# Softmax times values: who copies the last rows, when the last head's first bank is normalised, and how its scores are cut into loads

## The chip, the cores and the metric

The kernel runs on one core of one Trainium2 chip. The metric is the device time of one execution in microseconds (us), lower is better. A kernel is run several times and the median is given; executions differ by a few tenths of a microsecond, up to about one. The profile is one execution, with its own span from the first to the last instruction, 1.7 to 2.9 us below the device time of the same run.

Names of the engines: TensorE (PE in the profile, PEld for its weight loads), VectorE (DVE), ScalarE (ACT), GpSimd (POOL), and SyncE (SP), which issues all transfers.

## The reference

```python
def reference(scores, v):            # scores 8x12x1024x1024, v 8x12x1024x64, fp32
    scores_max = np.max(scores, axis=-1, keepdims=True)
    attn = np.exp(scores - scores_max)
    attn = attn / (np.sum(attn, axis=-1, keepdims=True) + 1e-8)
    return np.matmul(attn, v).astype(np.float32)
```

There are 96 heads (8 times 12), numbered 0 to 95 below. A head has 1024 rows of 1024 scores; the kernel handles them as 8 "rows" r = 0 to 7 of 128x1024 scores, half a megabyte each.

## The kernel before

A loop makes 24 passes of four heads, k = 0 to 3. The last pass has heads 92 to 95. For each row: ScalarE takes exp (no maximum is subtracted), TensorE transposes eight 128x128 blocks into PSUM (psT), VectorE copies them to SBUF (pt), and TensorE multiplies eight blocks by v, with a column of ones that gives the sums. Products run two rows behind the transposes (LAG). Four rows fill a PSUM bank; when it is full, VectorE inverts the sums and multiplies twice (two TENSOR_TENSOR, one for each half of the partitions).

```python
    def normalise(k, st, first, last):
        psO = psO_whole if k % 2 == 0 else psO_banks[first]
        ...
        nc.vector.reciprocal(out=recip, in_=psO[:, :, :, D : D + 1])
        for t in range(T):
            ...
            nc.vector.tensor_tensor(out=rows..., in0=psO[part, :, :, 0:D], in1=recip[part]..., op=mult)

    def finish(u):                       # the products of one row
        ...
        for c in range(C):
            nc.tensor.matmul(out=bank[:, g * M : (g + 1) * M], lhsT=pt[...], rhs=st["vones"][:, c, 0:M], ...)
        if k % 2 == 1:
            if g == G - 1:
                normalise(k, st, b, b + 1)
        elif r == R - 1:
            normalise(k, st, 0, R // G)
        ...

    def load_next(k, n0):
        if k < AHEAD - 2:
            load(k, (n0 + (AHEAD + k)) % BH, cond=n0 < BH - AHEAD)

    # last(n0), in the pass before the last: loads of heads 94 and 95, in parts of so many rows
                load(AHEAD - 2, BH - 2, (4, 4))
                load(AHEAD - 1, BH - 1, (2,))
                store(n0, AHEAD - T)
                load(AHEAD - 1, BH - 1, (2, 2, 1, 1), 2)

    # heads(n0), for every head k and row r
                if r % EB == 0:
                    rows = 1 if k == AHEAD - 1 and r == R - EB else EB      # EB = 2 rows in one exp
                    for g in range(0, EB, rows):
                        nc.scalar.activation(out=p_nat[...], in_=s_bufs[k][...], func=EXP)
                for c in range(C):
                    nc.tensor.transpose(out=psT[...], in_=p_row[...], identity=order16[:])
                pt = take(pt_bufs)
                nc.vector.tensor_copy(out=pt[:], in_=psT[:])
                pending.append((n0, k, r, pt, st))
                if len(pending) > LAG:
                    finish(pending.pop(0))
```

The softmax here doesn't subtract the row's maximum and nothing guards it: scores larger than these inputs give would overflow.

## Time and profile before

| what | value |
|---|---|
| device time, median of 3 runs (range) | 1064.57 us (1064.50 to 1064.79) |
| span of the profiled run | 1062.5 us |
| transfers | 453 MB in packets, mean 426 GB/s (HBM read and written: 461 MB, 434 GB/s over the span) |
| busy | ScalarE 69%, TensorE 68%, VectorE 64%, GpSimd 23% |
| last scores (row 7 of head 95) landed | 1052.02 us |
| first half of the last store issued | 1057.94 us |

How to read it: the transfers fill the span up to the last slice, so whatever an engine has to do before about 1050 us is hidden unless it reaches into the tail. A change that moves no bytes is worth only what it moves between the landing of the last scores and the last store. In the prediction below, L numbers are lines of the kernel; a timeline line gives start, busy time, engine, line, operation, output and input, and how often; in brackets the engine's idle time before it and what seems to have ended it.

### The profile page before, as it was taken

The page shows a single profiled execution, that of the slowest core. Times are in us where ns is not written, and L with a number is a line of the kernel's source. Part 1 is how long each engine was busy: PE and PEld are TensorE (multiplying, and loading weights), DVE is VectorE, ACT ScalarE, POOL GpSimd, SP SyncE. Part 2 cuts the span into 40 slices and gives each one's busy share as a digit, 9 for nine tenths or more (in the row PEclk, how much of TensorE's full clock was granted, in tenths as well). Part 3 has the DMA queues.
Part 4 walks back from the last instruction along what each step waited for, and adds up shares of the span by engine and source line. Part 5 has one row for each costly group of instructions (what it writes and reads, how often), then busy time and mean ns, then how long its engine had stood idle before and what let it go on. Part 6 is the DMA issues. An engine that isn't in the chain of part 4 may idle for free.

```text
span 1062.5 us, 32878 instructions
## 1 busy us (share of the span) xinstructions
PE 722.2 (68%) x12288; PEld 679.8 (64%) x12288; DVE 682.4 (64%) x1205; ACT 735.7 (69%) x432; POOL 243.5 (23%) x406
## 2 busy tenths in 40 slices
PE   2766766667766767666676666767667676667676
PEld 2765766657666667666676656757666576666675
DVE  1766666757566666666676656766667566666667
ACT  3766776666767668576675866767666677666686
POOL 3123212131121311212112221122121311203113
PEclk9888888888789798887888988888888988887989
DMA  9999999999999999999999999999999999999996
GB/s 398 429 418 434 429 434 434 432 435 432 431 429 432 430 432 435 434 433 432 435 424 434 433 429 435 427 441 433 432 432 427 433 429 435 434 433 433 432 427 257
DMA packets 25060, 453.06 MB, mean 426 GB/s; under 512 B 2784, under 2 KB 2784, under 8 KB 9312
## 3 DMA queue, kind: packets, MB, share of 16 engines
q1 hardware_dynamic: 25056, 453.00, 99.3%
q8 instruction: 4, 0.07, 0.0%
HBM read 436.21 MB, written 25.17 MB: 434 GB/s over the span
## 4 chain that ended last, share of the span: by engine, by line
DMA 61%; PE 15%; PEld 5%; ACT 5%; DVE 4%; issue 3%; POOL 3%; SPq 1%; POOLq 1%; ACTq 0%; PEldq 0%
DMA s_nat<-in_scores_dram 61%; PE psT L265 8%; PE psO L144 6%; ACT p_nat L253 5%; DVE pt L271 4%; PEld L265 3%; POOL vones L210 3%; PEld L144 2%; PE psO_whole L144 2%; SPq L201 1%; SPq L189 0%; POOLq L210 0%; POOLq L227 0%; POOLq L288 0%; POOLq L316 0%
## 5 line engine op out<-in xcount | busy, mean ns | idle before, releaser
L253 ACT ACTIVATE p_nat<-s_nat 128x2048 f16<-128x2048 f32 (+1 forms) x408 | 704.9, 1800 | 219.3 <-DMA s_nat<-in_scores_dram 192.2
L265 PE MATMUL psT<-order,p_nat 128*128 128x128 f16 x6144 | 565.0, 247 | 262.6 <-ACT p_nat L253 261.7
L271 DVE COPY pt<-psT 128x1024 f16<-128x1024 f16 x768 | 519.5, 690 | 348.4 <-PE L144 126.7
L265 PEld LDWEIGHTS <-p_nat 128*128 128x128 f16 x6144 | 448.6, 124 | 284.2 <-ACT p_nat L253 281.8
L210 POOL CAST vones<-v_sb 32x512 f16<-32x512 f32 x400 | 242.8, 607 | 815.9 <-PE L265 315.9
L144 PEld LDWEIGHTS <-pt 128*128 128x128 f16 x6144 | 303.9, 107 | 92.9 <-DVE pt L271 89.2
L144 PE MATMUL psO<-vones,pt 128*128 128x65 f16 x3072 | 183.2, 202 | 59.9 <-DVE pt L271 59.6
L144 PE MATMUL psO_whole<-vones,pt 128*128 128x65 f16 x3072 | 189.3, 209 | 12.3 <-DVE pt L271 11.9
L253 ACT ACT_TABLE_LOAD x24 | 30.8, 1283 | 98.5 <-DMA s_nat<-in_scores_dram 81.7
L128 DVE TENSOR_TENSOR out_sb<-psO,recip 64x256 f32<-64x256 f32 x192 | 81.2, 423 | 6.0
L128 DVE TENSOR_TENSOR out_sb<-psO_whole,recip 64x512 f32<-64x512 f32 x96 | 66.0, 688 | 3.1
L123 DVE RECIPROCAL recip<-psO 128x4 f32<-128x4 f32 x96 | 17.0, 177 | 17.2 <-PE psO L144 17.2
L123 DVE RECIPROCAL recip<-psO_whole 128x8 f32<-128x8 f32 x48 | 9.5, 198 | 0.0
L71 DVE MEMSET vones<- 128x16 f16 x4 | 0.2, 72 | 0.8 <-PEq L305 0.8
L62 DVE CAST order<-ident 128x128 f16<-128x128 f32 x1 | 0.2, 227 | 0.4 <-POOL ident masks.py:199 0.4
masks.py:199 POOL TENSOR_SCALAR_AFFINE_SELECT ident<-ident 128x128 f32<-128x128 f32 x1 | 0.3, 292 | 0.1
masks.py:197 POOL MEMSET ident<- 128x128 f32 x1 | 0.2, 204 | 0.3 <-POOLq L305 0.3
L305 POOL MEMSET const-float32-0.0<- 128x1 f32 x1 | 0.1, 98 | 0.3 <-issue 0.3
L305 POOL MEMSET const-bfloat16-1.0<- 128x1 bf16 x1 | 0.1, 100 | 0.0
L305 POOL MEMSET const-uint8-127<- 128x1 uint8 x1 | 0.1, 100 | 0.0
L305 POOL MEMSET const-float32-1.0<- 128x1 f32 x1 | 0.1, 98 | 0.0
## 6 DMA issues: line engine op xcount, KB each, us to landing
s_nat<-in_scores_dram SPq DMA_DIRECT2D x96, 4096.0 KB, 32.2
v_sb<-in_v_dram SPq DMA_DIRECT2D x24, 1024.0 KB, 18.4
out_dram<-out_sb SPq DMA_DIRECT2D x47, 512.0 KB, 27.6
s_nat<-in_scores_dram SPq DMA_DIRECT2D x2, 2048.0 KB, 33.4
s_nat<-in_scores_dram SPq DMA_DIRECT2D x3, 1024.0 KB, 27.4
s_nat<-in_scores_dram SPq DMA_DIRECT2D x2, 512.0 KB, 20.7
out_dram<-out_sb SPq DMA_DIRECT2D x2, 256.0 KB, 2.0
```

Source lines behind the costliest of these rows:

```text
L62: nc.vector.tensor_copy(out=order16[:].rearrange("p (t j) -> p t j", t=T), in_=ident32[:].rearrange("p (j t) -> p t j", t=T),)
L71: nc.vector.memset(vo[:, :, D : D + 2], 1.0)
L123: nc.vector.reciprocal(out=recip, in_=psO[:, :, :, D : D + 1])
L128: nc.vector.tensor_tensor(out=rows.rearrange("j (b g) d -> j b g d", g=G), in0=psO[part, :, :, 0:D], in1=recip[part].to_broadcast([W, last ...
L144: nc.tensor.matmul(out=bank[:, g * M : (g + 1) * M], lhsT=pt[:, c * P : (c + 1) * P], rhs=st["vones"][:, c, 0:M], start=(c == 0), stop=(c ...
L201: nc.sync.dma_start(out=v_sb[:].rearrange("x h s l d -> x (h s l d)"), in_=rows[bass.ds(n // AHEAD, 1)].rearrange("o x y -> (o x) y"),)
L210: nc.gpsimd.tensor_copy(out=vones_bufs[k][s * Q : (s + 1) * Q, :, 0:D].rearrange("i (h l) d -> i h l d", l=L), in_=v_sb[k * Q : (k + 1) * ...
L253: nc.scalar.activation(out=p_nat[:, g : g + rows, :].rearrange("p r (x v) -> p x r v", v=Q * L), in_=s_bufs[k][:, r + g : r + g + rows, :] ...
L265: nc.tensor.transpose(out=psT[:, c * P : (c + 1) * P], in_=p_row[:, c // L, c % L, :], identity=order16[:],)
L271: nc.vector.tensor_copy(out=pt[:], in_=psT[:])
L305: nc = _bacc.Bacc("TRN2", target_bir_lowering=False, num_devices=1)
```

## The change

Its intent is to shorten the tail. ScalarE, done with its exps, copies row 6 of a pass's last head, and VectorE is free for row 7's copy; the first bank of that head is normalised behind row 7's copy instead of ahead of it; and the very last head comes in parts of 3,2,1,1,1 rows, with exps of single rows from row 2 on.

```diff
-    def normalise(k, st, first, last):
+    def normalise(k, st, first, last, behind=None):
...
-        nc.vector.reciprocal(out=recip, in_=psO[:, :, :, D : D + 1])
+        inverse = nc.vector.reciprocal(out=recip, in_=psO[:, :, :, D : D + 1])
+        if behind is not None:
+            after(inverse, behind)
...
-            if g == G - 1:
+            if g == G - 1 and (b > 0 or k < AHEAD - 1):
                 normalise(k, st, b, b + 1)
...
-                load(AHEAD - 1, BH - 1, (2,))
+                load(AHEAD - 1, BH - 1, (3,))
                 store(n0, AHEAD - T)
-                load(AHEAD - 1, BH - 1, (2, 2, 1, 1), 2)
+                load(AHEAD - 1, BH - 1, (2, 1, 1, 1), 3)
...
-                    rows = 1 if k == AHEAD - 1 and r == R - EB else EB
+                    rows = 1 if k == AHEAD - 1 and r > 0 else EB
...
-                nc.vector.tensor_copy(out=pt[:], in_=psT[:])
+                if k == AHEAD - 1 and r == R - 2:
+                    nc.scalar.copy(out=pt[:], in_=psT[:])
+                else:
+                    copy = nc.vector.tensor_copy(out=pt[:], in_=psT[:])
+                if k == AHEAD - 1 and r == R - 1:
+                    normalise(k, st, 0, 1, copy)
```

## The prediction

> **What bounds the kernel now.** I read the page first: the slices of the span, the DMA queues, the waits of ScalarE; then only the last 15 us of the timeline.
>
> ```profile
> DMA  9999999999999999999999999999999999999996
> ...
> q1 hardware_dynamic: 25056, 453.00, 99.3%
> ...
> L253 ACT ACTIVATE p_nat<-s_nat 128x2048 f16<-128x2048 f32 (+1 forms) x408 | 704.9, 1800 | 219.3 <-DMA s_nat<-in_scores_dram 192.2
> ...
> out_dram<-out_sb SPq DMA_DIRECT2D x2, 256.0 KB, 2.0
> ```
>
> The 16 DMA engines are full in all slices but the last. In the packets I find no moment between 20 and 1045 us with fewer than 12 of the 16 at work. ScalarE, the busiest compute engine, is busy 69% and spends 192 us of its idle time waiting for scores. So 1045 us are set by 453 MB of traffic, and what compute does there has slack. The change moves no bytes. It can change the time only in what follows the last scores.
>
> The trace's landing records give the last head (number 95) in its parts of 2,2,2,1,1 rows: rows 0-1 complete at 1043.38 us, then the store of the heads before at 1044.69, rows 2-3 at 1047.13, rows 4-5 at 1049.54, row 6 at 1050.77, row 7 at 1052.02. A row takes 1.22 us. The span ends at 1062.5, so the tail after the last row is 10.5 us. The timeline there:
>
> ```profile
> 1049.64 3.81 ACT L253 ACTIVATE p_nat<-s_nat 128x2048 f16<-128x2048 f32 x3 [0.49 <-PE L265]
> 1050.82 0.69 DVE L128 TENSOR_TENSOR out_sb<-psO_whole,recip 64x512 f32<-64x512 f32 x1
> ...
> 1051.54 2.48 DVE L271 COPY pt<-psT 128x1024 f16<-128x1024 f16 x4
> ...
> 1053.94 0.18 DVE L123 RECIPROCAL recip<-psO 128x4 f32<-128x4 f32 x1
> ...
> 1054.24 0.69 DVE L271 COPY pt<-psT 128x1024 f16<-128x1024 f16 x1
> ...
> 1054.96 0.88 DVE L128 TENSOR_TENSOR out_sb<-psO,recip 64x256 f32<-64x256 f32 x2
> ...
> 1055.87 0.69 DVE L271 COPY pt<-psT 128x1024 f16<-128x1024 f16 x1
> 1056.61 0.31 PEld L144 LDWEIGHTS <-pt 128*128 128x128 f16 x8 [1.32 <-DVE pt L271]
> ...
> 1057.28 0.18 DVE L123 RECIPROCAL recip<-psO 128x4 f32<-128x4 f32 x1 [0.72 <-PE psO L144]
> 1057.49 0.88 DVE L128 TENSOR_TENSOR out_sb<-psO,recip 64x256 f32<-64x256 f32 x2
> ```
>
> What to see: ScalarE is done with its last exp at 1049.64+3.81 = 1053.45. From 1050.1 on VectorE runs without a pause: it normalises head 94 (until 1051.51), then copies rows 2 to 5, inverts bank 0, copies row 6 (1054.24), multiplies bank 0 (1054.96 to 1055.84), and only then copies row 7 (1055.87). TensorE waits 1.32 us for that copy. Row 7's product, its normalising and a store follow, then the fixed teardown. VectorE, not the last exp, sets the tail: row 7's transposes have long been there (their slice ends at 1054.36). The releaser named for the exp at 1049.64 is a matmul that had long ended; it is row 5's landing at 1049.54.
>
> **What the Trainium skill says.** "ScalarE: Activation LUTs", section "What ACT_TABLE_LOAD costs", gives an ACTIVATE with immediates 186 ns + 0.833 ns an element and an overlap of 93 ns back to back: 1039 ns at 1024 elements. The trace has 1043 ns for the exp of one row, and 1051.46 to 1052.41 between two starts, 0.95, so it agrees. Its section "Table sets" has copy in every set, so the new copy should need no table load; the built instruction list indeed has one load per pass, as before.
> "VectorE: DVE Perf Modes", "Side-by-side": a 16-bit copy at two elements a cycle is (512+8+150)/0.96 = 698 ns; the trace has 690. So a copy on ScalarE costs 0.35 us more than on VectorE, but beside it.
> "PSUM — Partial Sum Buffer", "Specifications", lets both engines read PSUM at full rate in different banks. Rows 6 and 7 lie in different transpose buffers of one bank each; no run yet shows it.
> "DMA: Bandwidth & Descriptors", "Anatomy of one DMA", has some 2 us of fixed cost; the last 256 KB stores take 2.0 from issue to landing. That stays.
>
> **The change part by part.**
> 1. Parts of 3,2,1,1,1, and exps of one row from row 1 pair onward (six where two were). Rows 0-2 complete at 1043.38+1.22 = 1044.60; the exp of rows 0-1 starts at 1044.67 today because ScalarE is busy until then, so nothing is lost. Rows 3-4 land at 1044.69+1.22+2.44 = 1048.35, row 5 at 1049.57, rows 6 and 7 as before. Exp of row 2 runs 1046.5 to 1047.5; row 3 starts at 1048.45; rows 4, 5, 6, 7 follow every 0.95, at 1049.40, 1050.35, 1051.30, 1052.25, the last ending at 1053.29. Gain against 1053.45: 0.16, and not on VectorE's chain.
> 2. ScalarE copies row 6, after its last exp. VectorE loses one 0.69 copy.
> 3. The inverse and the two products of bank 0 (0.18 + 0.88) move from ahead of row 7's copy to behind it.
> 4. In the built order VectorE now copies row 2 between the inverse and the products of head 94. That copy, and row 7's, wait for VectorE's own previous instruction; today such copies (row 6 of this head, for one) start 0.12 to 0.27 after the one before, the others 0.09 before its end.
>
> VectorE's new chain, from 1050.07, where head 94's inverse ends now as then: row 2's copy 1050.19 to 1050.88; two products of 0.69, 1050.91 to 1052.32; rows 3, 4, 5 at 1052.35, 1052.95, 1053.55, ending 1054.24 (today the same work ends at 1054.02: +0.22). Row 7's copy needs its transposes, and TensorE takes them in fixed order behind the product of row 4, which waits for row 4's copy (1053.65): product from 1053.71, transposes from 1053.96, and 0.71 from the first transpose to the copy (1023.63 to 1024.34 in the timeline): 1054.67. It ends at 1055.36, against 1056.56 today: 1.20 gained. Then bank 0, now exposed: inverse 1055.28 to 1055.46, products to 1056.37. Row 7's product starts at 1055.41 and releases the inverse 0.66 later (1056.62 to 1057.28 today) at 1056.07, so VectorE is later: inverse of bank 1 at 1056.40, first product 1056.61 to 1057.03. Today it ends at 1057.91. The gain is 0.88: 1.20 minus 0.32 in which bank 0 outlasts row 7's product.
> ScalarE's copy: row 6's transposes are split round the product of row 3, which waits for row 3's copy (1053.04): done about 1053.75, copy 1053.8 to 1054.85, product from 1054.9, 0.5 before row 7's. It is beside the path.
> The first of the two last stores is issued as its product ends, the second 0.68 later by the queue's pace, landing 2.0 after; both shift by 0.88, as does the teardown (VectorE's and GpSimd's ends move along). 1064.57 - 0.88 = 1063.69.
> In the 23 other passes ScalarE gets one more copy and three more starts, about 1.3 us, where it waits 3.45 us for scores at the start of each next pass: zero.
>
> **Rivals.**
> A. The copy of row 7 is bound by its exp alone: ending at 1053.29, transposes from 1053.35, copy at 1054.05, bank 0 done by 1055.8; a gain near 1.5, 1063.1. For it: the change aims at this. Against: VectorE is solid from 1050.1, and head 94's products still stand before row 3.
> B. ScalarE's copy takes the place of the removed wait: it stands behind the last exp and row 6's late transposes. It has 0.5 of slack before row 7's product, and 0.33 more since VectorE comes later; only a copy above 1.8 us would cost. At 2.5 us the gain would be near 0.2: 1064.4.
> C. The tail shifts but the span doesn't, as another chain ends last: GpSimd's four casts end at 1060.02, released by the last product, which shifts 1.2. They end before the stores (1060.67) and still will.
> D. The extra work at the end of each pass delays the loads or adds 0.1 us a pass: +2, 1066. Against: three loads queued, 32.2 us from issue to landing, with 9.7 us for one.
>
> **Range and chances.** The sum says 1063.7. Half of the gain rests on VectorE gaps of 0.1 to 0.3 us, so +-0.4; runs differ by 0.3; rival A stretches the low side. Range 1063.1 to 1064.4. 2% are 21 us, twice the whole tail, so "within 2%" is nearly sure.
>
> **What would show it right or wrong.** Loads landing within 0.2 of 1052.0; row 7's copy on VectorE starting near 1054.7 (1054.0 would be rival A); ScalarE's copy near 1.04 us with no table load; the two inverses within 1.2 us of each other; first last store issued near 1057.1. Wrong would be a DMA gap before 1045, or TensorE waiting for ScalarE's copy ahead of its last product.

## The result, and the profile after

The changed kernel took 1064.22 us (median of 6 runs, 1063.69 to 1064.56), the kernel before in the same rounds 1064.59 us (6 runs, 1064.39 to 1064.93). The ratio is 0.9996, with a 95% interval of 0.9983 to 1.0009. (Ratios here are the mean time of one kernel's fast runs over that of the other's of the same rounds, so not quite the ratio of the medians.) That is "same", inside the predicted range, but the difference of the medians is 0.37 us where 0.88 had been summed up. A second set, told below, gave 0.33. Neither set is clear of noise by its interval.

Spans scatter less: from span to device time it is anything from 1.73 to 2.86 us, in runs of one and the same kernel. In the three later calls the kernel before has spans of 1062.5 to 1063.8 us (27 runs, median 1062.7). The changed kernel has 1061.9 to 1062.5 in the first set (6 runs, median 1062.1) and 1062.0 to 1063.1 in the second (5 runs, median 1062.2, where the kernel before has 1062.8 in the same call; four of the five lie below all nine of it). So a gain of some 0.5 to 0.6 us stands out of the scatter of the spans, and the traces show where it comes from.

The page of the changed kernel: the same lines as before, and the new copy on ScalarE.

```profile
DMA  9999999999999999999999999999999999999996
...
q1 hardware_dynamic: 25056, 453.00, 99.4%
...
L255 ACT ACTIVATE p_nat<-s_nat 128x2048 f16<-128x2048 f32 (+1 forms) x456 | 709.4, 1630 | 218.6 <-DMA s_nat<-in_scores_dram 192.2
...
L275 ACT COPY pt<-psT 128x1024 f16<-128x1024 f16 x24 | 24.3, 1012 | 44.9 <-PE psT L267 21.7
...
out_dram<-out_sb SPq DMA_DIRECT2D x2, 256.0 KB, 2.0
```

The transfers are as they were, ScalarE still waits 192.2 us for scores, and its new copies of 1012 ns cost nothing outside the tail. Row 7 of the last head landed at 1052.05 us, against 1052.02.

Its timeline in the tail:

```profile
1050.60 0.69 DVE L277 COPY pt<-psT 128x1024 f16<-128x1024 f16 x1 [0.15 <-PE L146]
...
1051.32 1.41 DVE L130 TENSOR_TENSOR out_sb<-psO_whole,recip 64x512 f32<-64x512 f32 x2
...
1052.76 1.88 DVE L277 COPY pt<-psT 128x1024 f16<-128x1024 f16 x3
...
1054.44 1.01 ACT L275 COPY pt<-psT 128x1024 f16<-128x1024 f16 x1 [1.11 <-PE L267]
...
1055.40 0.69 DVE L277 COPY pt<-psT 128x1024 f16<-128x1024 f16 x1 [0.76 <-PE psO L146]
...
1056.01 0.17 DVE L123 RECIPROCAL recip<-psO 128x4 f32<-128x4 f32 x1
...
1056.21 0.88 DVE L130 TENSOR_TENSOR out_sb<-psO,recip 64x256 f32<-64x256 f32 x2
...
1057.12 0.18 DVE L123 RECIPROCAL recip<-psO 128x4 f32<-128x4 f32 x1
1057.34 0.88 DVE L130 TENSOR_TENSOR out_sb<-psO,recip 64x256 f32<-64x256 f32 x2
```

The order is the predicted one: row 2, head 94's products, rows 3 to 5 (ending at 1054.64), row 7, bank 0, bank 1. But the reader is to see the 0.76 us in the row 7 line. VectorE is idle from 1054.64 to 1055.40, in the middle of what had been taken for its own chain, and it is TensorE that it waits for. Row 7's copy starts 0.47 us earlier than in the kernel before (1055.87), not 1.20. And nothing stands between the products of bank 0 and the inverse of bank 1 (1056.21+0.88 = 1057.09, then 1057.12): bank 0, moved behind the copy, now delays bank 1. The first half of the last product ends at 1057.75, against 1057.91 before.

**Where TensorE really is.** Ends of matrix multiplies in a profile are modelled. The trace has something firmer: every matrix multiply and every weight load counts up a semaphore when it is done, and the time of each count is recorded. Set beside the timeline for a row's eight transposes (us, worked out from the trace's semaphore records):

```
                       slices in the timeline   last transpose counted   copy starts
before, row 7 of 95      1053.75 to 1054.36            1055.18             1055.87
after,  row 0 of 95      1047.59 to 1048.23            1048.72             1048.74
after,  row 1 of 95      1048.29 to 1048.90            1049.62             1049.64
after,  row 2 of 95      1048.99 to 1049.61            1050.58             1050.60
after,  row 7 of 95      1054.37 to 1054.98            1055.38             1055.40
```

The four copies of the changed kernel start 0.02 us after the last count: they wait for TensorE, which is up to 1.2 us further behind than its slices look. (The recorded texts below have these counts 0.03 earlier: they were read one count short. That the sixteenth count of a row is the one is seen where TensorE has stood idle before a row: in the kernel before, the first count after the pause at 1023.63 us is at 1023.75, the sixteenth at 1024.31, and the copy starts at 1024.34.) The counts never come closer than 0.029 us in the whole trace. In full clock they come every 0.030, so a load and its multiply take 0.060, a row's transposes and products (16 pairs) 0.96 us. Between 1038.2 and 1055.0 us, 560 counts of 0.030 would fit; the changed kernel has 560, the kernel before 554. In the changed kernel TensorE is saturated from there to its last product, without a pause in its counts. In the kernel before it pauses twice: 0.18 us at 1051.64, for an exp of two rows, and 0.64 us at 1056.13, for VectorE's copy of row 7. Whether the array or the counting sets this pace, the traces do not tell.

**A second thing that the timeline hides**: TensorE's clock. The view by windows, of the kernel before:

```profile
core 0: us, PE busy (x) PEld busy (x) DVE busy (x) ACT busy (x) POOL busy (x), PEclk, DMA share, GB/s
1022.93:1029.77 6.84, 5.74 (x90) 5.48 (x91) 4.22 (x8) 6.06 (x4) 2.22 (x4) 0.75 0.95 405
```

and of the changed kernel, the same stretch:

```profile
1022.93:1029.77 6.84, 6.07 (x68) 5.91 (x69) 3.44 (x6) 6.12 (x4) 1.32 (x3) 0.50 0.96 408
```

The column to read is the granted clock after the engines: 0.75 and 0.50. TensorE runs at half clock for windows of 3.4 or 6.8 us, which fall differently in every run. Here one of 6.8 us ended at 1029.8 in the changed kernel, one of 3.4 us at 1027.6 in the kernel before, and so 68 multiplies were begun in the stretch instead of 90. The lost time reaches the tail, because TensorE has no pause in which to catch up.

I therefore measure every tail from two marks: the landing of head 93, 22 us before the last row's, and the end of TensorE's last pause before its saturated stretch, which I call its entry (to be exact, the second count after that pause). It comes 7.82 us after that landing in the kernel before and 8.17 after it in the changed kernel. From entry to the end of the first product of bank 1 (the moment the first half of the last store can go), the kernel before takes 20.13 us and the changed one 19.60. So the change gained 0.53. Row 7's copy comes 0.85 us earlier from entry: 0.67 for which VectorE had held it back behind its finished transposes (1055.87 less 1055.18, less the 0.02), and 0.18 by which TensorE no longer pauses at 1051.64. Of that, bank 0 takes 0.28 back behind the last product. And the profiled run gave 0.35 back at entry, after its longer half-clock window.

### The profile page after: what moved, and what is told of

Read it like the earlier page. It is cut to its first block, busy times and chain, and to the rows that moved or that the text cites. A ratio compares the mean times of both kernels' runs of the same rounds, so it can differ in the third digit from the quotient of the medians.

```text
span 1062.5 us, 33096 instructions
## 1 busy us (share of the span) xinstructions
PE 722.9 (68%) x12288; PEld 677.3 (64%) x12288; DVE 664.5 (63%) x1181; ACT 764.5 (72%) x504; POOL 244.2 (23%) x406
## 4 chain that ended last, share of the span: by engine, by line
DMA 62%; PE 16%; ACT 5%; PEld 5%; issue 3%; POOL 3%; DVE 3%; SPq 1%; POOLq 1%; ACTq 0%; DVEq 0%
DMA s_nat<-in_scores_dram 62%; PE psT L267 8%; PE psO L146 6%; ACT p_nat L255 5%; POOL vones L212 3%; PEld L267 3%; DVE pt L277 3%; PEld L146 2%; PE psO_whole L146 1%; SPq L203 1%; SPq L191 0%; POOLq L212 0%; POOLq L229 0%; POOLq L297 0%; POOLq L325 0%
## 5 line engine op out<-in xcount | busy, mean ns | idle before, releaser
L255 ACT ACTIVATE p_nat<-s_nat 128x2048 f16<-128x2048 f32 (+1 forms) x456 | 709.4, 1630 | 218.6 <-DMA s_nat<-in_scores_dram 192.2
L277 DVE COPY pt<-psT 128x1024 f16<-128x1024 f16 x744 | 502.8, 690 | 382.6 <-PE L146 117.6
L146 PE MATMUL psO<-vones,pt 128*128 128x65 f16 x3072 | 178.4, 202 | 41.0 <-DVE pt L277 29.6
L275 ACT COPY pt<-psT 128x1024 f16<-128x1024 f16 x24 | 24.3, 1012 | 44.9 <-PE psT L267 21.7
```

What stands on the lines that cost most here:

```text
L146: nc.tensor.matmul(out=bank[:, g * M : (g + 1) * M], lhsT=pt[:, c * P : (c + 1) * P], rhs=st["vones"][:, c, 0:M], start=(c == 0), stop=(c ...
L255: nc.scalar.activation(out=p_nat[:, g : g + rows, :].rearrange("p r (x v) -> p x r v", v=Q * L), in_=s_bufs[k][:, r + g : r + g + rows, :] ...
L275: nc.scalar.copy(out=pt[:], in_=psT[:])
L277: copy = nc.vector.tensor_copy(out=pt[:], in_=psT[:])
```

## The experiments

Theory T: TensorE's pace from head 93's landing bounds the tail. Theory V: VectorE's chain does, as the prediction had it. Three calls of the chip, each with its own runs of the kernel before (medians 1064.54, 1064.71 and 1064.65 us, 9 runs each). One table for all; "entry" is measured from the landing of head 93, the other three from entry, in us. Outputs are right except in the two kernels marked wrong.

| kernel | median (range) us | last half-clock window ended | entry | row 7's copy | last product counted | bank 1's first product ends |
|---|---|---|---|---|---|---|
| before | 1064.59 (1064.39 to 1064.93) | 1027.6 | 7.82 | 18.09 | 19.48 | 20.13 |
| after | 1064.22 (1063.69 to 1064.56) | 1029.8 | 8.17 | 17.24 | 18.66 | 19.60 |
| parts_only | 1064.56 (1064.30 to 1065.16) | 1028.0 | 7.83 | 18.10 | 19.49 | 20.14 |
| undo_copy | 1063.94 (1063.79 to 1065.04) | 1029.1 | 8.02 | 17.24 | 18.66 | 19.60 |
| undo_order | 1063.96 (1063.77 to 1064.73) | 1028.4 | 7.82 | 17.53 | 18.91 | 19.57 |
| relief_after (wrong) | 1063.51 (1063.25 to 1064.26) | 1026.7 | 7.82 | 16.74 | 18.15 | 19.10 |
| after_again | 1064.38 (1063.78 to 1064.87) | 1026.7 | 7.83 | 17.24 | 18.66 | 19.60 |
| split_after | 1064.67 (1064.64 to 1065.41) | 1029.6 | 7.82 | 17.24 | 18.66 | 19.60 |
| split_undo_order | 1064.98 (1064.45 to 1065.50) | 1029.7 | 7.82 | 17.52 | 18.91 | 19.56 |
| burden_after (wrong) | 1067.61 (1066.84 to 1067.93) | 1028.5 | 7.88 | 19.16 | 20.58 | 21.52 |
| lag3_after | 1064.00 (1063.66 to 1064.54) | 1029.6 | 8.09 | 16.82 | 18.66 | 19.32 |
| lag3_undo_order | 1063.97 (1063.63 to 1065.26) | 1028.3 | 7.82 | 16.82 | 18.66 | 19.32 |

split_before (1065.70 us, 1065.39 to 1065.82) has no such pause and is told in its own place.

### relief_after: less for TensorE

```diff
-        for c in range(C):
+        chunks = C // 2 if k == AHEAD - 2 else C
+        for c in range(chunks):
...
-                stop=(c == C - 1),
+                stop=(c == chunks - 1),
```

> The changed kernel, but head k=2 of each pass takes four of its eight products a row (a wrong result on purpose): 32 matrix multiplies, by the 0.060 us that the semaphore records put between two, 1.92 us less of TensorE in the last pass ahead of the last head, no VectorE, ScalarE or DMA work less. Theory T (TensorE's own rate bounds the tail: it completes without a pause from about 1043 to 1056.8 us and row 7's copy waits for row 7's transposes): row 7's copy starts about 0.6 us after the last exp ends instead of 2.1, the first of the last stores is issued 1.0 to 1.5 us earlier after the last landing, time 1062.7 to 1063.3. Theory V (the prediction's: VectorE's chain of copies and products bounds it): the chain starts no earlier, gain under 0.3, time 1063.9 to 1064.3.

Wrong on purpose, and measured 1063.51 us: between the two ranges, so both missed by the clock. In the trace, row 7's copy starts 1.26 us after the last exp ends (2.08 in the changed kernel), the first product of bank 1 ends 0.50 earlier after entry, and the first of the last stores goes 0.85 us earlier after row 7's landing (4.88 against 5.73). Taking work from TensorE alone shortens the tail, for which theory V allowed under 0.3 us, and VectorE stands idle for 1.59 us before row 7's copy; but only 0.50 of the 1.92 us taken away shows, because TensorE then pauses 1.4 us more than in the changed kernel, for exps and copies. The other engines are close behind.

### undo_copy: row 6 back to VectorE

```diff
-                if k == AHEAD - 1 and r == R - 2:
-                    nc.scalar.copy(out=pt[:], in_=psT[:])
-                else:
-                    copy = nc.vector.tensor_copy(out=pt[:], in_=psT[:])
+                copy = nc.vector.tensor_copy(out=pt[:], in_=psT[:])
```

> The changed kernel with row 6 copied by VectorE again. Theory T: row 7's transposes complete no earlier or later; VectorE has row 6's copy done about 0.2 us after they are, so row 7's copy and all behind it shift by 0.3 to 0.5 us: about as slow as before, 1064.4 to 1064.7. Theory V: VectorE's chain gets 0.69 plus a gap of 0.27 longer, about 0.5 to 0.9 us lost, 1064.7 to 1065.1.

Both theories had this slower; it was not (1063.94 us). The timeline:

```profile
1053.06 1.88 DVE L273 COPY pt<-psT 128x1024 f16<-128x1024 f16 x3
...
1055.09 0.69 DVE L273 COPY pt<-psT 128x1024 f16<-128x1024 f16 x1 [0.15 <-PE L146]
```

VectorE makes rows 4, 5 and 6 in one stretch, without the gap that I had put before row 6, ends at 1054.94, and still waits 0.15 us for row 7's transposes (counted at 1055.07). From entry, every column of the table is that of the changed kernel. ScalarE's copy bought nothing: it fills a time in which VectorE would have been idle.

### undo_order: bank 0 where it was

```diff
-            if g == G - 1 and (b > 0 or k < AHEAD - 1):
+            if g == G - 1:
                 normalise(k, st, b, b + 1)
...
-                if k == AHEAD - 1 and r == R - 1:
-                    normalise(k, st, 0, 1, copy)
```

> The changed kernel with the first bank normalised where it was, ahead of row 7's copy; ScalarE still copies row 6. Theory T: the 1.06 us of inverse and products fit between row 5's copy (end 1054.65) and row 7's transposes (complete 1055.35) but for about 0.3 us, and bank 0 no longer stands between the last product and its inverse: within 0.15 us of the changed kernel, 1064.1 to 1064.3. Theory V: row 7's copy starts 0.7 us later, the end is 0.3 to 0.5 us later: 1064.5 to 1064.7.

1063.96 us, faster than either theory said, and 19.57 against 19.60 from entry: the same, as theory T has it. Row 7's copy is 0.29 us later, since bank 0's products stand before it, and the last product 0.25 later; but the inverse of bank 1 then follows that product by 0.02 us instead of 0.30. What the order wins at one end it loses at the other.

### parts_only: the kernel before with the new parts and exps

```diff
-                load(AHEAD - 1, BH - 1, (2,))
+                load(AHEAD - 1, BH - 1, (3,))
                 store(n0, AHEAD - T)
-                load(AHEAD - 1, BH - 1, (2, 2, 1, 1), 2)
+                load(AHEAD - 1, BH - 1, (2, 1, 1, 1), 3)
...
-                    rows = 1 if k == AHEAD - 1 and r == R - EB else EB
+                    rows = 1 if k == AHEAD - 1 and r > 0 else EB
```

> The kernel before with only the parts of 3,2,1,1,1 rows and the exps of one row from the second pair on. Theory T and theory V alike: the last exp ends 0.1 to 0.2 us earlier, but row 7's copy still stands behind row 6's copy and the first bank's products, and row 2's copy takes a gap of 0.2 more: 0 to 0.2 us slower than before, 1064.6 to 1064.8. If the parts are the gain: 1064.2.

1064.56 us beside 1064.54 of the kernel before; from entry 20.14 and 20.13. The last exp does end earlier after row 7's landing (1.29 us against 1.43), and nothing comes of it. By themselves the parts are neutral. They do take away TensorE's pause of 0.18 us (row 7's transposes are counted 17.22 us after entry, as in the changed kernel, and 17.40 in the kernel before), but behind VectorE's chain that doesn't show. The change without the new parts was not run; it may lack these 0.18 us.

So with the new parts in place, row 6 on VectorE and bank 0 ahead of row 7 together cost 0.5 us; taking away either is worth all of it, and the second adds nothing.

### after_again: the changed kernel once more

> The changed kernel once more, for the spread and for another phase of TensorE's half-speed windows. Measured from row 7's landing, the first half of the last store's product ended at 5.70 in the first profile, in which the last half-speed window ended at 1029.8 us. Theory T: TensorE is behind by what such a window leaves over; if the window ends before 1028.5 the product ends at 5.3 to 5.45, if after 1029.5 at 5.6 to 5.75. If phase has no part in it, 5.7 again. Time 1063.7 to 1064.5.

1064.38 us beside 1064.71. The half-clock window ended at 1026.7 this time, the product ended 5.15 us after row 7's landing (5.70 in the first profile). That is under the expected 5.3 to 5.45, because the last row itself landed late (1052.47), which is why I changed to measuring from entry: entry is 7.83 instead of 8.17, and from entry all four columns are equal to the first profile's to 0.01 us. What goes with entry over the twelve profiles of the table is how long before head 93's landing the last window ended: where it was 1.2 us or more, entry is 7.82 to 7.88 (split_after and split_undo_order are among these, as head 93 landed later there); where it was 0.7, 0.4 and 0.2 us, in undo_copy, lag3_after and after, entry is 8.02, 8.09 and 8.17. That is a pattern, not an experiment: nothing here sets the windows.

### split_before, split_after, split_undo_order: an earlier start for head 92

```diff
-            load(k, (n0 + (AHEAD + k)) % BH, cond=n0 < BH - AHEAD)
+            parts = (R // 2, R // 2) if k == 0 else (R,)
+            load(k, (n0 + (AHEAD + k)) % BH, parts, cond=n0 < BH - AHEAD)
```

> The kernel before with the scores of head k=0 of each pass loaded in two parts of four rows, so that in the last pass its exps start at about 1018 us instead of 1021.7 and TensorE doesn't pause 2 to 3 us between 1020.8 and 1025.7. Nothing else changes, outputs stay right. Theory T: TensorE is 1 to 2 us ahead when the last head comes; row 7's copy then stands behind VectorE's chain alone: first product of bank 1 ends 5.0 to 5.4 after row 7's landing instead of 5.9, time 1063.7 to 1064.2. Theory V: nothing in the tail starts earlier, 1064.4 to 1064.8. If the extra transfer a pass costs DMA time: over 1065.

> The changed kernel with the same two parts for head k=0. Theory T: with TensorE out of the way the change has the effect that the prediction summed up: row 7's copy 2.2 to 2.6 after row 7's landing (3.35 without the parts), the product ends at 4.5 to 4.9, time 1063.0 to 1063.5, 0.5 to 0.9 under split_before. If ScalarE's copy at the end of a pass holds up the exps of the next head (it ended at 1020.24 in the changed kernel), the lead is 1 us smaller than in split_before and the gain under 0.4. Theory V: same as the changed kernel, 1064.0 to 1064.4.

> As split_after, with bank 0 normalised ahead of row 7's copy as before the change. Theory T: row 5's copy ends about 1053.1, bank 0 is done by about 1054.3, row 7's copy starts 2.3 to 2.6 after row 7's landing, and after its product only bank 1 is left: product ends at 4.2 to 4.6, time 1062.7 to 1063.2, the best of all. Theory V as in the prediction's step 3: 0.3 to 0.4 slower than split_after.

1065.70, 1064.67 and 1064.98 us: outside the ranges of both theories in all three; only the branch "over 1065" of split_before came true. Two things were wrong in the theories' ranges. First, the extra transfer of every pass is not free: head 93 landed at 1030.9 us and row 7 at 1052.9 to 1053.0, some 0.8 later than in most other profiles, although the same bytes moved and no moment between 20 and 1045 us has fewer than 12 packets in flight. The packet records show where it went: a packet of 32 KB took 1.214 us on average, two of 16 KB 1.222, and the packets' times come to 1057.5 to 1057.7 us on each of 16 engines, against 1055.4 in the kernel before and 1055.7 and 1056.0 in the two profiles of the changed one. Second, the lead is not kept. In split_before the exps of head 92 do start at 1019.15 instead of 1021.66, but ScalarE and TensorE then just wait for head 93, which still comes whole: TensorE's counts pause for 1.2 us at 1031.95. (A half-clock window, 1034.3 to 1037.8 us, also fell into the stretch that leads to its tail.) In split_after there is no lead at all: ScalarE's copy of the pass before ends at 1020.56, and the exps of head 92 start behind it at 1022.05, no earlier than without the split. It and split_undo_order have an entry of 7.82 and the columns of the kernels without the split, so they tell nothing new of the tail. What split_before shows is that a lead on head 92 alone is given back while TensorE waits for head 93. Splitting head 93 too was not run: I expected the next pass's first load to wait for the last store then, which no run here shows.

### burden_after: more for TensorE

```diff
-        for c in range(C):
+        chunks = list(range(C)) + (list(range(C // 2)) if k == AHEAD - 2 else [])
+        for i, c in enumerate(chunks):
...
-                start=(c == 0),
-                stop=(c == C - 1),
+                start=(i == 0),
+                stop=(i == len(chunks) - 1),
```

> The changed kernel, but head k=2 of each pass takes four of its products a second time (a wrong result on purpose): 32 more matrix multiplies a pass, 1.92 us of TensorE at 0.060 each, nothing for VectorE, ScalarE and DMA. Theory T, now from head 93's landing on (TensorE has no pause worth naming from 2 us after that landing to its last product): the first product of bank 1 ends 29.3 to 29.7 us after head 93's landing instead of 27.4 (27.8 with a late half-speed window), time 1.6 to 2.0 over the changed kernel, 1065.9 to 1066.3. Theory V: VectorE has not a copy more to make, under 0.3 later, 1064.2 to 1064.6.

Wrong on purpose. From entry, the last product comes 1.92 us later (20.58 against 18.66), the very 32 pairs of 0.060, and bank 1's product 1.92 later (21.52 against 19.60). From head 93's landing it is 29.40 us, inside theory T's 29.3 to 29.7. VectorE's line for row 7:

```profile
1058.49 0.69 DVE L278 COPY pt<-psT 128x1024 f16<-128x1024 f16 x1 [1.11 <-PE psO L147]
```

VectorE has no copy more to make and is idle for 1.11 us before this one, again for TensorE. This is the run that decides between the theories for the changed kernel. The time, 1067.61 us, is 1.3 above what I had expected, because head 93 landed at 1031.44 us, 1.2 to 1.6 later than in the profiles without a split; why the longer products delay the loads of the passes before is left open.

### lag3_after and lag3_undo_order: row 7's transposes first

```diff
-                if len(pending) > LAG:
+                if len(pending) > (LAG + 1 if k == AHEAD - 1 and r > R // 2 else LAG):
```

> The changed kernel with the products of the last head three rows behind its transposes from row 5 on, not two, so that row 7's transposes come ahead of seven of row 4's eight products. The same instructions, only their order on TensorE. Theory T: TensorE's last product ends as before, 26.5 after head 93's landing, but row 7's copy starts 0.42 earlier and bank 0 is done when the last product is: the product of bank 1 ends 27.05 to 27.25 after head 93's landing instead of 27.42 (27.4 to 27.6 with a late window), time 0.2 to 0.4 under the changed kernel, 1063.8 to 1064.1. Theory V: row 7's copy follows VectorE's chain, which is unchanged: 0.0 to 0.1.

> As lag3_after with bank 0 normalised as before the change (its inverse comes ahead of row 7's copy, its products behind). Theory T: VectorE has the same work in the same 1.9 us between row 7's transposes and the last product, so the same within 0.1 us of lag3_after: 27.05 to 27.3 after head 93's landing.

The same instructions in another order on TensorE. Measured 1064.00 and 1063.97 us beside 1064.65. From entry the last product is where it was (18.66), row 7's copy 0.42 earlier (16.82), and bank 1's product ends at 19.32, 0.28 earlier, whichever way bank 0 goes. From head 93's landing that is 27.41 in lag3_after (entry 8.09 behind a late window) and 27.14 in lag3_undo_order, both as expected. The timeline of the latter:

```profile
1054.73 0.69 DVE L277 COPY pt<-psT 128x1024 f16<-128x1024 f16 x1 [0.24 <-PE L146]
1055.45 0.88 DVE L130 TENSOR_TENSOR out_sb<-psO,recip 64x256 f32<-64x256 f32 x2
...
1056.59 0.18 DVE L123 RECIPROCAL recip<-psO 128x4 f32<-128x4 f32 x1 [0.26 <-PE psO L146]
1056.81 0.88 DVE L130 TENSOR_TENSOR out_sb<-psO,recip 64x256 f32<-64x256 f32 x2
```

Row 7's copy and bank 0 are both done, and VectorE waits 0.26 us for the last product. This is the shortest tail of all kernels with right outputs, and it has come down to TensorE's stream and one bank's normalising. By the clock it is 0.7 us under the kernel before, which its interval (ratio 0.9996, 0.9983 to 1.0010) does not separate from zero, and level with undo_copy and undo_order. By the spans it is clear: 1061.7 to 1062.9 us (5 runs, median 1062.0) beside 1062.5 to 1062.9 (9 runs, median 1062.7), four of the five below all nine.

## Why the prediction was right or wrong

The time fell into the predicted range, near its upper end, and in part by luck: the range had room for any gain from 0.2 to 1.5 us, and the step that was to bring most of the 0.88 failed. What failed is TensorE's part in it.

- **Nothing but the tail matters: right for the transfers, wrong for TensorE.** What compute does before 1045 us was said to have slack, but TensorE has none from 1038 us on, and its backlog reaches the tail. The DMA rows of both pages agree, row 7 landed within 0.03 us, and the copies in the 23 other passes cost nothing. There ScalarE's slack turned out smaller than I had it: in the last pass but one the copy ended at 1020.24 and the next scores landed at 1020.31.
- **"VectorE, not the last exp, sets the tail: row 7's transposes have long been there (their slice ends at 1054.36)": this is the step that failed.** They were counted as done at 1055.18, and TensorE had been all but saturated for 17 us by then. The slices show modelled ends, and I took one for a fact. VectorE did set the tail of the kernel before, but of its hold on row 7's copy only 0.67 us was there to be won; then TensorE sets it, as it does in the changed kernel.
- **Row 7's copy at 1054.67, "0.71 from the first transpose to the copy": wrong.** It took 1.03 (1054.37 to 1055.40), because TensorE had a backlog. The 0.71 came from 1023.63 us, where it had just been idle. From entry, the copy gained 0.85 us where 1.20 was forecast, and the first last store was issued at 1057.78, not near 1057.1. Of the 0.73 us by which the copy came later than forecast, 0.38 is the later entry (1038.16 us, against 1037.78 in the kernel before).
- **The chain starts at 1050.07, "now as then": wrong by 0.37 us in the profiled run.** Head 94's inverse ended at 1050.44. In the second profile it began at 1050.12, where the first had 1050.25, although head 93 had landed 0.22 later. It goes with entry (from there it begins at 12.09 in both, and in the kernel before), and so with the half-clock windows, which the prediction did not mention.
- **VectorE's chain itself: right.** From head 94's inverse to the end of row 5's copy I had 1050.07 to 1054.24, 4.17; measured 1050.44 to 1054.64, 4.20.
- **"0.32 in which bank 0 outlasts row 7's product": right**, 0.28 to 0.30 us between the last product's count and the inverse.
- **ScalarE's copy: right** in length (1.01 us in the tail), and in needing no table load. The timeline shows TensorE waiting 0.27 us for it, which the prediction called a sign of being wrong; but the counts run on at 0.030 there, the wait lies in TensorE's backlog. That it is beside the path was right, and undo_copy shows that it might as well be absent. The 1039 and 698 ns that the prediction works out from the skill's figures are estimates; an exp of 1024 elements took 1043 here and VectorE's copy 690. The two engines' reading of PSUM side by side, of which the prediction had no run, shows in lag3_undo_order: ScalarE's copy took its usual 1.01 us (1053.71 to 1054.72), beside two of VectorE's (until 1054.40).
- **The sum.** Of 0.88, the trace shows 0.53 from entry; the medians of device time 0.37 and 0.33, those of the spans 0.6. Entry, 0.35 later in the first profile, goes with the half-clock phase. How much of it stands in the medians, too few profiles tell.
- **The rivals.** None was the right one. A had the exp as the next bound, B ScalarE's copy. TensorE's own pace was not on the list, because 68% busy and pauses of up to 1.3 us in its line looked like slack.

## What to carry to other kernels

In a tail, find out which engine is saturated by its completions and not by its slices: a consumer that starts a constant 0.02 us after the producer's last count is waiting for it, however early the slices end. Where one engine is saturated, taking work off another helps only up to the moment the saturated one delivers; then look at the order of its own work (row 7's transposes first, another 0.28 us). And measure small gains in the tail from a mark inside the trace: without the splits and the burden, row 7's landing moved by 0.55 us from run to run and entry by 0.35, while the columns from entry repeated to 0.01. Where there is no trace, the span is the better clock here.

## What the Trainium skill lacked or had wrong

- "Perfetto Trace Analysis", section "Per-engine timelines", does say that TensorE's end times are estimated from an instruction's size; I did not weigh it. It gives no size: here the last transpose of a row was counted 0.4 to 1.2 us after its slice had ended (row 7 before: 1054.36 and 1055.18; row 4 after: 1051.27 and 1052.50).
- "TensorE: Matmul & The Clock Gate", section "Back-to-back issue gap", gives some 81 ns per multiply for a stream of loads and multiplies of 128 columns. These runs show 0.060 us a pair, for 128 columns and for 65, over 17 us without a pause.
- The same page, section "What's actually happening", has half clock after an idle window of some 3.4 us. The windows here are 3.41 or 6.83 us long, which agrees with that unit, and their phase differs from run to run, as the section also says. "Idle" does not agree: in the kernel before, 66 such windows begin between 25 and 1050 us, and in the 3.41 us before each TensorE made a median of 44 counts of the 114 that fit, none at all in only two cases. That the phase of the windows can reach a tail 20 us later (entry 7.82 or 8.17) stands on no page.
- No page has what one more transfer costs in a queue that is never empty: cutting one load of each pass in two, with the same bytes, moved head 93's landing by some 0.8 us over 23 passes, about 0.035 each.
